# Stick-breaking attention of a head pair: the two heads in step on the two halves of TensorE's rows, float32 value products into one bank, and another split of the eight PSUM banks

## The chip, the cores and the metric

The kernel runs on one core of a Trainium2 chip. The metric is device time in microseconds (us) of one execution; the median of three runs stands for a kernel.

## What is computed

A model of two layers over 528 positions (16 meta tokens and 512 inputs), width 1024. In each layer an input projection feeds three mixers side by side: stick-breaking attention (6 heads of 64), retention (6 heads of 64) and an S5 state-space mixer (256 channels). Their outputs go through one output projection, and a gated feed-forward block of width 2816 follows. The change is about the attention, of which this is the core (per block of 128 queries):

```python
z = jnp.einsum('bhqd,bhkd->bhqk', qb, kb).astype(jnp.float32) * scale
mask = (s_idx[None, :] < t_idx[:, None]) & (s_idx[None, :] >= PAD_FRONT)
log1m = jnp.where(mask, jax.nn.log_sigmoid(-z), 0.0)
between = lax.cumsum(log1m, axis=3, reverse=True) - log1m
w = jnp.where(mask, jnp.exp(jax.nn.log_sigmoid(z) + between), 0.0)
outs.append(jnp.einsum('bhqk,bhkd->bhqd', w.astype(vb.dtype), vb))
```

Everything is float32.

## The kernel before, in words

All activations lie with channels on the 128 partitions and the 528 positions in the free dimension. The large products (input, output and feed-forward projections, tiles `pj`) are made of three matmuls in the reduced type float32r each: both operands are split into a high and a low part (`xh`, `xl`, `wh`, `wl`), and high by high, low by high and high by low are added up in PSUM (`mm3`). With 264 columns each half of the positions has its own bank, so a projection block holds two banks.

The mixers are written as Python generators (`tasks`). After each three matmuls of a projection, `tick` lets up to six tasks take one step, so that mixer work is emitted between projection matmuls; at last Tile's scheduler sets the order on each engine, which is then fixed, and each engine runs its own list in order. Banks are counted by hand: `free` holds a count of banks (`BANKS`, line 32: 5 of the 8) that all mixers share through `banks(n)` and `freed(n)`, and one of attention groups in flight (`GROUPS`, 7). The other three banks are left to the projections. Before the output projection reads a mixer's result, `drain` (line 202) empties the tasks that are still needed; `OUT_PARTS` (line 41) sets which results each third of the output projection reads, and retention is last in both layers.

Attention (`sb_group`, line 816, and `sb_head`, line 857): three pairs of heads per layer; the pair's queries `sq` and keys `sk` are one tile each, head 0 on partitions 0 to 63 and head 1 on 64 to 127. Each head is a lane of its own (`sb_lane(0)`, `sb_lane(1)`, line 1092), and the two lanes run independently of each other. A head's keys and queries fall into three groups: A (272 + 144 + 16 columns), B2 (256 + 144 + 16) and B1 (256 + 256). For a group:

- a bf16 mask product starts the bank `z` (A and B2 only; `identb` is its weight), and float32 matmuls of 64 rows (one head's half of `sk` and `sq`) add the scores;
- ScalarE and VectorE make the softplus `sp`, which is split into `hi` and `lo`; products with `tri` and `ones` (float32r) add the sums over later keys into the same bank;
- ScalarE takes the exponential `e` and frees the bank; `e` is split into `hi` (ScalarE) and `lo` (POOL) by `slow_split`.

The value product `av` of a head takes `hi` and `lo` as two float32r matmuls against a 128-column weight: the 64 columns of the value's high part and the 64 of its low part side by side (`vparts`, line 895, makes them from the transposed values). ScalarE then copies partitions 64 to 127 of the bank (`avl`), VectorE adds them to partitions 0 to 63 into the head's half of `sbo`, and `sbo` is split once more for the output projection.

Retention (`ret_pair`, line 932) also works on a pair: its scores `sc` are float32 matmuls of 64 rows, issued head 0, head 1, head 0, ..., each head in its own bank, and its inner products `ro` are float32 matmuls with 64-column weights, both heads into one bank, also by turns. It takes three banks at once for `sc`, two for `ro`. A head norm (`headnorm`, line 424) takes two banks.

Of the kernel before, what the change touches and what calls it, by code (L numbers as in the profile page):

```python
# [24 lines left out]
NT_SLOTS = 60  # L25
# [6 lines left out]
BANKS = 5  # L32
GROUPS = 7
# [55 lines left out]
def hybrid_kernel(ctx, tc, A, out, dbg=None):  # L89
# [81 lines left out]
    free = {"bank": BANKS, "group": GROUPS}  # L171
# [644 lines left out]
    def sb_group(q, k, r, g, gi, place, hl, ws):  # L816
# [37 lines left out]
        freed(1)  # L854
        ws[gi] = yield from slow_split(e, n, G)

    def sb_head(q, k, v, hh, o):

        r = slice(64 * hh, 64 * hh + 64)
        def weights(groups):  # L860
            hl, ws = {}, {}
            place = {j: (gi, o0, q0) for gi, g in enumerate(groups) for j, q0, q1, o0 in g}
            for gi, g in enumerate(groups):
                spawn(sb_group(q, k, r, g, gi, place, hl, ws), now[0][1])
            return ws

        started = []
        sets = ((G_A,), (G_B2, G_B1))
        yield from take("group", len(sets[0]))
        started.append(weights(sets[0]))  # L870
        for groups in sets:
            ws = started[-1]
            if groups is sets[0]:
                yield from take("group", len(sets[1]))
                started.append(weights(sets[1]))
            yield lambda: len(ws) == len(groups)
# [8 lines left out]
            ws.clear()  # L885
            yield
            freed(len(groups), "group")
            lo = tt("avl")
            SC.copy(out=lo[0:64, :qb - qa], in_=av[64:128, :qb - qa])
            yield  # L890
            V.tensor_tensor(out=o[r, qa:qb], in0=lo[0:64, :qb - qa], in1=av[0:64, :qb - qa], op=ALU.add)
            yield
            freed(1)

    def vparts(vt):

        v = vp.tile([P, 1280], F32R, tag="v", name=nm("v"))
        v4 = v.rearrange("p (j h c) -> p j h c", h=2, c=P)
        for j0, nj in ((0, 4), (4, 1)):
# [5 lines left out]
            pv = ps[:, :P * nj].rearrange("p (j h d) -> p j h d", h=2, d=64)  # L905
            for hh in range(2):
                SC.copy(out=v4[:, j0:j0 + nj, hh, 0:64], in_=pv[:, :, hh, :])
            yield
            for hh in range(2):
                V.tensor_tensor(out=v4[:, j0:j0 + nj, hh, 64:128], in0=pv[:, :, hh, :],  # L910
                                in1=v4[:, j0:j0 + nj, hh, 0:64].bitcast(F32), op=ALU.subtract)
            yield
            freed(1)
        return v4
# [17 lines left out]
    def ret_pair(l, p, q, k, vt, gate, res):  # L932
# [38 lines left out]
        yield from banks(3)  # L971
        pss, ps2 = [bank("sc"), bank("sc")], bank("sc")

        def score(hh, j):
            r, n = slice(64 * hh, 64 * hh + 64), P if j < 4 else NM
            c = slice(P * j, P * j + n)
            mm(pss[hh][:, c] if j < 4 else ps2[:n, :n], lhsT=k[r, c], rhs=q[r, c], start=True, stop=True)

        def kept_last(sc):
            V.tensor_tensor(out=sc[:NM, 512:528], in0=ps2[:NM, :NM], in1=keep[:NM, :NM], op=ALU.mult)  # L980
        score(0, 4)
# [4 lines left out]
        kept_last(scs[0])  # L986
# [3 lines left out]
        score(1, 4)  # L990
        yield
        kept_last(scs[1])
        yield
        freed(3)
# [68 lines left out]
    for l in range(LAYERS):  # L1063
# [15 lines left out]
        def after(n, p, t, l=l, got=got):  # L1079
# [7 lines left out]
            elif n == "sv":  # L1087
                yield lambda: p < 2 or (("done", p - 2, 0) in got and ("done", p - 2, 1) in got)
                t = yield from vparts(t)
            got[n, p] = t  # L1090

        def sb_lane(hh, l=l, got=got, mix=mix):
            for p in range(3):
                yield lambda: all((n, p) in got for n in ("sq", "sk", "sv"))
                if ("sbo", p) not in got:
                    got["sbo", p] = tt("sbo")
                yield from sb_head(got["sq", p], got["sk", p], got["sv", p], hh, got["sbo", p])
                got["done", p, hh] = True
                if ("done", p, 1 - hh) in got:
                    dump(f"sb{l}{p}", got["sbo", p])  # L1100
                    mix[p] = yield from slow_split(got["sbo", p])
# [18 lines left out]
        spawn(sb_lane(0))  # L1120
        spawn(sb_lane(1))
# [160 lines left out]
```

## Time and profile before

| | |
|---|---|
| median of three runs | 1380.3 us (1379.69 to 1380.94) |
| the profiled execution's own time | 1384.1 us |
| its span, first to last instruction | 1382.4 us |
| mean granted TensorE clock | 0.995 |
| busy: PE (matmul) / DVE / ACT / POOL | 1352.0 / 806.3 / 618.1 / 514.6 us |

PE is TensorE's matmuls, PEld its weight loads, DVE VectorE, ACT ScalarE, POOL GpSimd. Matmuls are pipelined: the duration of one reaches into the next ones, so what a matmul costs is read from its start to the next one's start. A float32 matmul shows as two records, a float32r one as one. The rows of the timeline merge equal neighbours: start, time from the first start to the last end, engine, line, operation, output<-inputs, tile shape, count of records.

### The profile page before, as it was taken

The page shows a single profiled execution, that of the slowest core. Times are in us where ns is not written, and L with a number is a line of the kernel's source. Part 1 is how long each engine was busy: PE and PEld are TensorE (multiplying, and loading weights), DVE is VectorE, ACT ScalarE, POOL GpSimd, SP SyncE. Part 2 cuts the span into 40 slices and gives each one's busy share as a digit, 9 for nine tenths or more (in the row PEclk, how much of TensorE's full clock was granted, in tenths as well). Part 3 has the DMA queues.
Part 4 walks back from the last instruction along what each step waited for, and adds up shares of the span by engine and source line. Part 5 has one row for each costly group of instructions (what it writes and reads, how often), then busy time and mean ns, then how long its engine had stood idle before and what let it go on. Part 6 is the DMA issues. An engine that isn't in the chain of part 4 may idle for free.

```text
span 1382.4 us, 22757 instructions
## 1 busy us (share of the span) xinstructions
PE 1352.0 (98%) x9188; PEld 1241.3 (90%) x9188; DVE 806.3 (58%) x1312; ACT 618.1 (45%) x1002; POOL 514.6 (37%) x624
## 2 busy tenths in 40 slices
PE   6999999999899999999999999999999999999998
PEld 6989999999899999999999998998788888888886
DVE  8874858767456445534567386555585543554453
ACT  5456676555252233312354664874354422332231
POOL 5685648322899112201234534562232210220120
PEclk9999999999999999999999999999999999999999
DMA  4221212323221322322232220123232332233223
GB/s 156 70 74 50 78 46 71 94 77 108 84 78 59 109 92 92 92 92 88 78 110 70 71 93 32 70 59 90 86 105 95 102 93 92 92 96 103 92 79 104
DMA packets 38985, 118.27 MB, mean 86 GB/s; under 512 B 4960, under 2 KB 5472, under 8 KB 38880
## 3 DMA queue, kind: packets, MB, share of 16 engines
q1 hardware_dynamic: 38880, 116.82, 25.9%
q8 instruction: 72, 1.18, 0.3%
q14 instruction: 33, 0.27, 0.1%
HBM read 111.46 MB, written 2.10 MB: 82 GB/s over the span
## 4 chain that ended last, share of the span: by engine, by line
PE 75%; DVE 4%; POOL 3%; issue 1%; ACT 1%; SPq 0%; DMA 0%; DVEq 0%; ACTq 0%
PE pj L133 67%; PE z L133 4%; PE ro L133 1%; PE hps L133 1%; PE av L133 1%; PE yps L133 1%; DVE wl L121 1%; DVE y L121 0%; DVE fr L121 0%; POOL st L121 0%; POOL py L121 0%; PE sc L133 0%; POOL gx L121 0%; POOL bb L121 0%; PE rtp L139 0%
## 5 line engine op out<-in xcount | busy, mean ns | idle before, releaser
L133 PE MATMUL pj<-xh,wh 128*128 128x264 f32 (+1 forms) x1792 | 447.8, 310 | 14.6 <-ACT wh L121 5.3
L133 PE MATMUL pj<-xl,wh 128*128 128x264 f32 (+1 forms) x1792 | 450.5, 311 | 1.6 <-DVE xl L121 1.6
L133 PE MATMUL pj<-xh,wl 128*128 128x264 f32 (+1 forms) x1792 | 447.5, 310 | 1.6 <-DVE wl L121 1.6
L121 ACT CAST wh<-wr 128x1024 fp32r<-128x1024 f32 (+3 forms) x209 | 205.9, 987 | 412.7 <-PE pj L133 378.6
L133 PEld LDWEIGHTS pj<-xh,wh 128*128 128x128 f32 x1792 | 296.8, 190 | 33.1 <-issue 7.4
L133 PEld LDWEIGHTS pj<-xl,wh 128*128 128x128 f32 x1792 | 297.2, 190 | 20.2 <-DVE xl L121 2.4
L133 PEld LDWEIGHTS pj<-xh,wl 128*128 128x128 f32 x1792 | 297.0, 191 | 18.7 <-DVE wl L121 1.8
L121 DVE TENSOR_TENSOR wl<-wr,wh 128x1024 fp32r<-128x1024 f32 (+3 forms) x166 | 249.6, 1505 | 72.4 <-ACT wh L121 72.1
L133 PE MATMUL pj<-hi,wh 128*128 128x264 f32 (+1 forms) x720 | 192.5, 322 | 0.0
L133 PE MATMUL pj<-lo,wh 128*128 128x264 f32 (+1 forms) x720 | 192.4, 321 | 0.0
L133 PE MATMUL pj<-hi,wl 128*128 128x264 f32 (+1 forms) x720 | 191.8, 321 | 0.1
L121 POOL TENSOR_TENSOR up<-ga,up 128x528 f32<-128x528 f32 (+1 forms) x44 | 62.0, 1409 | 344.8 <-DVE up L121 344.7
L121 POOL TENSOR_TENSOR wl<-wr,wh 128x1024 fp32r<-128x1024 f32 (+2 forms) x43 | 96.8, 2252 | 137.3 <-ACT wh L121 117.8
L121 DVE TENSOR_TENSOR h<-h,pj 128x264 f32<-128x264 f32 (+1 forms) x144 | 69.4, 510 | 134.7 <-PE pj L133 134.5
L133 PEld LDWEIGHTS pj<-hi,wl 128*128 128x128 f32 x720 | 119.5, 188 | 11.0 <-DVE wl L121 0.5
L133 PEld LDWEIGHTS pj<-hi,wh 128*128 128x128 f32 x720 | 119.4, 188 | 10.9 <-ACT wh L121 0.6
L133 PEld LDWEIGHTS pj<-lo,wh 128*128 128x128 f32 x720 | 119.4, 188 | 10.5
L121 POOL TENSOR_TENSOR lo<-ga,hi 128x528 fp32r<-128x528 f32 (+1 forms) x44 | 59.0, 1340 | 158.3 <-ACT hi L121 158.2
L121 DVE TENSOR_TENSOR up<-pj,R 128x264 f32<-128x264 f32 (+1 forms) x66 | 32.1, 514 | 95.2 <-PE pj L133 95.2
L121 ACT ACTIVATE si<-si,bias 128x528 f32<-128x528 f32 (+1 forms) x44 | 32.1, 730 | 95.3 <-DVE si L121 95.3
L121 DVE TENSOR_TENSOR ga<-si,up 128x528 f32<-128x528 f32 (+1 forms) x44 | 31.7, 719 | 73.8 <-ACT si L121 58.7
L121 POOL TENSOR_TENSOR lo<-sp,hi 128x432 fp32r<-128x432 f32 (+2 forms) x36 | 46.4, 1301 | 34.4 <-ACT hi L121 34.3
(228 smaller groups left out, 1710.9 us busy)
## 6 DMA issues: line engine op xcount, KB each, us to landing
wr<-in_w_in_dram SPq DMA_DIRECT2D x45, 512.0 KB, 3.4
wr<-in_w_gate_dram SPq DMA_DIRECT2D x44, 512.0 KB, 3.4
wr<-in_w_up_dram SPq DMA_DIRECT2D x44, 512.0 KB, 3.4
wr<-in_w_down_dram SPq DMA_DIRECT2D x32, 512.0 KB, 3.5
wr<-in_w_out_dram SPq DMA_DIRECT2D x16, 384.0 KB, 3.2
wr<-in_w_down_dram SPq DMA_DIRECT2D x16, 384.0 KB, 3.1
rc<-in_rope_dram SPq DMA_DIRECT2D x12, 264.0 KB, 3.7
rs<-in_rope_dram SPq DMA_DIRECT2D x12, 264.0 KB, 3.8
```

The lines of the kernel that those rows point to most:

```text
L121: return f(*a, **k)
L133: nc.tensor.matmul(out, lhsT=lhsT, rhs=rhs, start=start, stop=stop, skip_group_check=more)
```

## The change

- **Scores.** `sb_scores` issues both heads' score matmuls by turns, head 0 (rows 0 to 63) into one bank, head 1 (rows 64 to 127) into another. One task per group and pair takes two banks for it, from a count of their own (`ZBANKS` = 4).
- **Value product.** `e` isn't split any more. `av` takes `e` and the values in float32: head 0 with the 64 weight columns that write partitions 0 to 63, head 1 with those that write 64 to 127, by turns, into one bank. The values are copied once as float32 (`by_keys` in place of `vparts`).
- **After it.** The bank holds both heads' rows already; ScalarE copies it as `hi`, VectorE subtracts to `lo`: the split for the output projection comes straight from PSUM, without `avl`, `sbo` and their split.
- **Banks.** `BANKS` 5 to 2 for everything but scores, `ZBANKS` 4, `GROUPS` 7 to 8 (counted per head). Retention's scores take two banks: the last 16 columns of both heads come first, in the same banks, and are read before the others are written.
- **Lanes.** One lane per pair; the next pair may start its groups when the value products of the last one's second set are reached.

```diff
-BANKS = 5
-GROUPS = 7
+BANKS = 2
+ZBANKS = 4
+GROUPS = 8
...
-    def sb_group(q, k, r, g, gi, place, hl, ws):
-
+    def sb_scores(q, k, g):
 
         n = width(g)
-        yield from banks(1)
-        zp = bank("z")
         m = masks.get(n)
+        zs = [bank("z"), bank("z")]
         if m is not None:
-            mm(zp[:, :n], lhsT=identb, rhs=m, start=True, stop=False)
+            for z in zs:
+                mm(z[:, :n], lhsT=identb, rhs=m, start=True, stop=False)
         for j, q0, q1, o0 in g:
-            mm(zp[:, o0:o0 + q1 - q0], lhsT=k[r, KT0[j]:KT0[j] + P], rhs=q[r, q0:q1],
-               start=m is None and j == g[0][0], stop=j == g[-1][0], more=m is None)
+            for hh, z in enumerate(zs):
+                r = slice(64 * hh, 64 * hh + 64)
+                mm(z[:, o0:o0 + q1 - q0], lhsT=k[r, KT0[j]:KT0[j] + P], rhs=q[r, q0:q1],
+                   start=m is None and j == g[0][0], stop=j == g[-1][0], more=m is None)
+        return zs
...
         SC.activation(e[:, :n], z, AF.Exp)
         yield
-        freed(1)
-        ws[gi] = yield from slow_split(e, n, G)
+        freed(1, "scores")
+        ws[gi] = e
...
+            def one(gi, g):
+                yield from take("scores", 2)
+                zs = sb_scores(q, k, g)
+                for hh in range(2):
+                    spawn(sb_group(zs[hh], g, gi, place, hl[hh], ws[hh]), now[0][1])
...
             for n, (gi, (j, q0, q1, o0)) in enumerate(todo):
-                for part in range(2):
-                    mm(av[:, q0 - qa:q1 - qa], lhsT=v[:, j, hh, :], rhs=ws[gi][part][:, o0:o0 + q1 - q0],
-                       start=n == 0 and part == 0, stop=n == len(todo) - 1 and part == 1)
...
+                for hh in range(2):
+                    mm(av[64 * hh:64 * hh + 64, q0 - qa:q1 - qa], lhsT=v[:, P * j + 64 * hh:P * j + 64 * hh + 64],
+                       rhs=ws[hh][gi][:, o0:o0 + q1 - q0], start=n == 0, stop=n == len(todo) - 1)
...
-            lo = tt("avl")
-            SC.copy(out=lo[0:64, :qb - qa], in_=av[64:128, :qb - qa])
-            yield
-            V.tensor_tensor(out=o[r, qa:qb], in0=lo[0:64, :qb - qa], in1=av[0:64, :qb - qa], op=ALU.add)
...
+            SC.copy(out=R_(hi[:, qa:qb]), in_=av[:, :qb - qa])
+            yield
+            V.tensor_tensor(out=R_(lo[:, qa:qb]), in0=av[:, :qb - qa], in1=hi[:, qa:qb], op=ALU.subtract)
...
-    def vparts(vt):
+    def by_keys(vt):
...
+            SC.copy(out=v[:, P * j0:P * (j0 + nj)], in_=ps[:, :P * nj])
...
-        yield from banks(3)
-        pss, ps2 = [bank("sc"), bank("sc")], bank("sc")
+        yield from banks(2)
+        pss = [bank("sc"), bank("sc")]
...
-        spawn(sb_lane(0))
-        spawn(sb_lane(1))
+        for p in range(3):
+            spawn(sb_lane(p))
```

How the order on PE changes, at three places. First, the scores of layer 0's first pair. Before (`z_1055` is one head's group B2, `z_1062` the other's, `z_1067` a group B1):

```order
L133 LDWEIGHTS identb
L133 MATMUL z_1055<-maskB_99,identb 128x416
L133 MATMUL z_1055<-sq_491,sk_494 128x256
L133 MATMUL z_1055<-sq_491,sk_494 128x144
L133 MATMUL z_1055<-sq_491,sk_494 128x16
L133 MATMUL pj_969<-xh_189,wh_796 128x264
L133 MATMUL pj_970<-xh_189,wh_796 128x264
```

Now (`z_913` and `z_914` are the two heads' banks):

```order
L134 LDWEIGHTS identb
L134 MATMUL z_913<-maskB_99,identb 128x416
L134 LDWEIGHTS identb
L134 MATMUL z_914<-maskB_99,identb 128x416
L134 MATMUL z_913<-sq_491,sk_494 128x256
L134 MATMUL z_914<-sq_491,sk_494 128x256
L134 MATMUL z_913<-sq_491,sk_494 128x144
L134 MATMUL z_914<-sq_491,sk_494 128x144
L134 MATMUL z_913<-sq_491,sk_494 128x16
L134 MATMUL z_914<-sq_491,sk_494 128x16
```

The two heads' score matmuls, which stood apart, now alternate. Score matmuls stand in 28 runs before (a run ends where another kind of matmul follows) and in 20 now. Second, a value product of set B. Before, one head:

```order
L133 MATMUL av_1873<-hi_1518,v_598 128x256
L133 MATMUL av_1873<-lo_1519,v_598 128x256
L133 MATMUL av_1873<-hi_1518,v_598 128x256
L133 MATMUL av_1873<-lo_1519,v_598 128x256
L133 MATMUL av_1873<-hi_1454,v_598 128x256
L133 MATMUL av_1873<-lo_1455,v_598 128x256
L133 MATMUL av_1873<-hi_1454,v_598 128x144
L133 MATMUL av_1873<-lo_1455,v_598 128x144
L133 MATMUL av_1873<-hi_1454,v_598 128x16
L133 MATMUL av_1873<-lo_1455,v_598 128x16
```

Now, both heads (`e_1379` and `e_964` are head 0's, `e_1383` and `e_968` head 1's):

```order
L134 MATMUL av_1639<-e_1379,v_594 64x256
L134 MATMUL av_1639<-e_1383,v_594 64x256
L134 MATMUL av_1639<-e_1379,v_594 64x256
L134 MATMUL av_1639<-e_1383,v_594 64x256
L134 MATMUL av_1639<-e_964,v_594 64x256
L134 MATMUL av_1639<-e_968,v_594 64x256
L134 MATMUL av_1639<-e_964,v_594 64x144
L134 MATMUL av_1639<-e_968,v_594 64x144
L134 MATMUL av_1639<-e_964,v_594 64x16
L134 MATMUL av_1639<-e_968,v_594 64x16
```

Ten matmuls for two heads stand in place of ten for one. They stand in 16 runs: in 4 of the 12 sets other work lies between the first matmul of head 0 and the rest. Third, group B1 of layer 0's second pair, now, with projection matmuls around it (`x2`: two equal rows):

```order
L134 MATMUL pj_1746<-xh_194,wh_1474 128x264
L134 MATMUL z_1821<-sq_560,sk_702 128x256 x2
L134 MATMUL pj_1747<-xh_194,wh_1474 128x264
L134 MATMUL pj_1746<-xl_195,wh_1474 128x264
L134 MATMUL pj_1747<-xl_195,wh_1474 128x264
```

Here one head's two matmuls stand alone; the other head's (`z_1822`) follow 22 rows later. Of the 18 groups this is the only one that is wholly apart; in two more B1 groups two of the four matmuls have no partner beside them.

## Rows read from the trace of the kernel before

**Rows 1.** The page: span, busy time per engine, PE and clock in 40 slices.

```profile
span 1382.4 us, 22757 instructions
PE 1352.0 (98%) x9188; PEld 1241.3 (90%) x9188; DVE 806.3 (58%) x1312; ACT 618.1 (45%) x1002; POOL 514.6 (37%) x624
PE   6999999999899999999999999999999999999998
PEclk9999999999999999999999999999999999999999
```

**Rows 2.** Waits of PE: who waited for whom, us in total, times, longest.

```profile
PE pj L133 <- DVE py L121: 2.0, 1, 2.0
PE ro L133 <- DVE sc L121: 1.6, 1, 1.6
PE av L133 <- POOL lo L121: 1.3, 1, 1.3
PE z L133 <- DVE u L121: 0.8, 1, 0.8
```

**Rows 3.** Timeline of PE, groups B2 and B1 of one head.

```profile
190.57 0.49 PE L133 MATMUL pj<-xl,wh 128*128 128x264 f32 x2
190.90 0.35 PE L133 MATMUL z<-maskB,identb 128*128 128x416 bf16 x1
191.18 2.03 PE L133 MATMUL z<-sq,sk 64*128 64x256 f32 x10
193.14 0.51 PE L133 MATMUL pj<-xh,wl 128*128 128x264 f32 x2
193.49 0.41 PE L133 MATMUL pj<-xh,wh 128*128 128x264 f32 x2
193.74 0.28 PE L133 MATMUL pj<-xl,wh 128*128 128x264 f32 x1
```

**Rows 4.** Timeline of PE, group A of one head.

```profile
903.75 1.09 PE L133 MATMUL z<-sq,sk 64*128 64x272 f32 x6
904.77 0.50 PE L133 MATMUL z<-hi,tri 128*128 128x512 f32 x1
```

**Rows 5.** Timeline of PE, retention's scores of both heads by turns.

```profile
254.52 0.41 PE L133 MATMUL pj<-xl,wh 128*128 128x264 f32 x2
254.86 1.30 PE L133 MATMUL sc<-rm,rm 64*16 64x16 f32 x18
256.09 0.51 PE L133 MATMUL pj<-xh,wl 128*128 128x264 f32 x2
```

**Rows 6.** Timeline of PE, seven of retention's inner products by turns.

```profile
260.33 1.09 PE L133 MATMUL ro<-sc,rv 128*64 128x128 f32 x14
261.35 0.71 PE L133 MATMUL ro<-rm,st 128*128 128x128 f32 x4
```

**Rows 7.** Timeline of PE, value products of one head: set A, set B.

```profile
121.72 0.28 PE L133 MATMUL av<-hi,v 128*128 128x272 f32 x1
...
122.33 0.49 PE L133 MATMUL pj<-xl,wh 128*128 128x264 f32 x2
...
131.88 0.28 PE L133 MATMUL av<-hi,v 128*128 128x256 f32 x1
...
132.95 0.49 PE L133 MATMUL pj<-xh,wh 128*128 128x264 f32 x2
```

**Rows 8.** Groups by line: work on e, of ACT and POOL.

```profile
L121 ACT ACTIVATE e<-z 128x512 f32<-128x512 f32 (+2 forms) x72 | 39.2, 546 | 37.3 <-PE z L133 35.7 <-POOL lo L121 0.9
L121 ACT CAST hi<-e 128x432 fp32r<-128x432 f32 (+2 forms) x36 | 20.0, 569 | 0.8
L121 POOL TENSOR_TENSOR lo<-e,hi 128x432 fp32r<-128x432 f32 (+2 forms) x36 | 44.5, 1247 | 31.9 <-ACT hi L121 31.9
```

**Rows 9.** Windows: PE busy, clock, DMA, around the first score products.

```profile
84.20:90.70 6.50, 6.50 (x26) 0.50 0.00 0
```

**Rows 10.** Timeline: layer 0's last head norm, then its result's two parts.

```profile
294.72 1.05 PE L133 MATMUL hps<-hsq,blk 128*128 128x264 f32 x4
300.58 0.64 ACT L121 CAST hi<-o 128x528 fp32r<-128x528 f32 x1 [1.21 <-DVE o L121]
302.02 0.69 DVE L121 TENSOR_TENSOR lo<-o,hi 128x528 fp32r<-128x528 f32 x1
```

More of the change, by code (lines that the diff above doesn't have):

```diff
@@ L24 @@
 HALF = T // 2
-NT_SLOTS = 60
+NT_SLOTS = 62
 AHEAD = 4
@@ L169, in spawn @@
         tasks.append([gen, at, None, None, 0.0])
-    free = {"bank": BANKS, "group": GROUPS}
+    free = {"bank": BANKS, "scores": ZBANKS, "group": GROUPS}
     def take(what, n):
@@ L853, in sb_group, with sb_pair @@
         yield
-        freed(1)
-        ws[gi] = yield from slow_split(e, n, G)
-    def sb_head(q, k, v, hh, o):
-        r = slice(64 * hh, 64 * hh + 64)
+        freed(1, "scores")
+        ws[gi] = e
+    def sb_pair(q, k, v, go, res):
         def weights(groups):
-            hl, ws = {}, {}
+            hl, ws = ({}, {}), ({}, {})
             place = {j: (gi, o0, q0) for gi, g in enumerate(groups) for j, q0, q1, o0 in g}
+            def one(gi, g):
[3 more added lines that the diff above has]
+                    spawn(sb_group(zs[hh], g, gi, place, hl[hh], ws[hh]), now[0][1])
             for gi, g in enumerate(groups):
-                spawn(sb_group(q, k, r, g, gi, place, hl, ws), now[0][1])
+                spawn(one(gi, g), now[0][1])
             return ws
@@ L868, in sb_head @@
         sets = ((G_A,), (G_B2, G_B1))
-        yield from take("group", len(sets[0]))
+        yield from take("group", 2)
         started.append(weights(sets[0]))
+        hi = lo = None
         for groups in sets:
@@ L873, in sb_head @@
             if groups is sets[0]:
-                yield from take("group", len(sets[1]))
+                yield from take("group", 4)
                 started.append(weights(sets[1]))
-            yield lambda: len(ws) == len(groups)
+            yield lambda: all(len(w) == len(groups) for w in ws)
+            if groups is sets[1]:
+                go()
             yield from banks(1)
@@ L904, in vparts @@
             yield
-            pv = ps[:, :P * nj].rearrange("p (j h d) -> p j h d", h=2, d=64)
-            for hh in range(2):
-                SC.copy(out=v4[:, j0:j0 + nj, hh, 0:64], in_=pv[:, :, hh, :])
-            yield
-            for hh in range(2):
-                V.tensor_tensor(out=v4[:, j0:j0 + nj, hh, 64:128], in0=pv[:, :, hh, :],
-                                in1=v4[:, j0:j0 + nj, hh, 0:64].bitcast(F32), op=ALU.subtract)
+            SC.copy(out=v[:, P * j0:P * (j0 + nj)], in_=ps[:, :P * nj])
             yield
             freed(1)
-        return v4
+        return v
     def rotate(t, p, which):
@@ L976, in score @@
             c = slice(P * j, P * j + n)
[L977 to L981, printed above, removed]
+            mm(pss[hh][:n, c if j < 4 else slice(0, n)], lhsT=k[r, c], rhs=q[r, c], start=True, stop=True)
+        for hh in range(2):
+            score(hh, 4)
+        yield
+        for sc, ps in zip(scs, pss):
+            V.tensor_tensor(out=sc[:NM, 512:528], in0=ps[:NM, :NM], in1=keep[:NM, :NM], op=ALU.mult)
+        yield
         for j in range(4):
@@ L1077, in scaled, with after @@
             return t
-        def after(n, p, t, l=l, got=got):
+        def after(n, p, t, l=l, got=got, mix=mix):
             yield
@@ L1087, in after, with sb_lane @@
             elif n == "sv":
-                yield lambda: p < 2 or (("done", p - 2, 0) in got and ("done", p - 2, 1) in got)
-                t = yield from vparts(t)
+                yield lambda: p < 2 or mix[p - 2] is not None
+                t = yield from by_keys(t)
             got[n, p] = t
[L1092 to L1101, printed above, removed]
+        def sb_lane(p, l=l, got=got, mix=mix):
+            yield lambda: all((n, p) in got for n in ("sq", "sk", "sv")) and (p == 0 or ("sb", p - 1) in got)
+            res = []
+            yield from sb_pair(got["sq", p], got["sk", p], got["sv", p], lambda: got.update({("sb", p): True}), res)
+            mix[p] = res[0]
         def ret_lane(l=l, got=got, mix=mix):
```

19 lines of the change are left out of this document (10 added, 9 removed).

## The prediction

> **What bounds the kernel now.** I read the page first: PE is busy for 98% of the span, in every slice after the first few, at full clock nearly throughout [rows 1]. The other engines are at 58% or less, so their work counts only where PE waits for it, and in the stretches with mixers PE waits little: the largest waits there are 2.0, 1.6, 1.3 and 0.8 us [rows 2]. So a change is worth what it takes off the list of PE's matmuls, plus or minus what PE waits. Next I priced matmuls from start to start in the timeline, since their own durations overlap.
>
> Scores of one head: groups B2 and B1 together take 193.14 - 191.18 = 1.96 us, and group A 904.77 - 903.75 = 1.02 us [rows 3, 4], in all 2.98 us for five 256-column matmuls or near it and the small ones. Twelve heads (three pairs, two layers) make 35.8 us. Value products of one head: set A 122.33 - 121.72 = 0.61 us, set B 132.95 - 131.88 = 1.07 us [rows 7], in all 1.68 us, times twelve 20.2 us. These 56 us are what the change rewrites.
>
> **What two halves cost in step.** The kernel has the pattern already, in retention. Sixteen records of 128-column scores, eight matmuls of the two heads by turns, lie in 256.09 - 254.86 = 1.23 us less some 0.14 us for the two 16-column records ahead of them: 1.09 us, 0.14 us for a matmul [rows 5]. The attention's scores, one head alone, cost 1.96 us for 256 + 144 + 16 + 256 + 256 = 928 columns, 2.1 ns a column, 0.27 us for 128 columns [rows 3]. So matmuls on the two row halves, standing beside each other, run at the same time: two for the price of one. For column halves the same: seven inner products of 128 columns take 261.35 - 260.33 = 1.02 us, 0.15 us each [rows 6]. I take it that 256 columns behave as 128 do; no row shows that length in step, and the bounds are no overlap (rival 1) and full overlap.
>
> **The change part by part.**
>
> *Scores.* With full overlap a pair costs what one head did: 6 x 2.98 = 17.9 us. The new order keeps partners apart in one B1 group (two extra matmuls) and half of two more (one extra each): four times 256 columns at 2.1 ns, 2.2 us. So 35.8 becomes 20.1 us: **-15.7 us**. The mask products stay as many as they were.
>
> *Value product.* One float32 matmul with 64 weight columns costs what a score matmul of the same width costs: two records, and rows 6 show 64 columns as quick as rows 5 show 64 rows. The widths are those of the scores, group for group (272 + 144 + 16 and 928 columns). So a pair costs 2.98 us in step, six pairs 17.9 us; four of the twelve sets have their first matmul apart, at 0.54 us each 2.2 us more. That is 20.1 us against 20.2 us: **0**. The float32 matmul takes twice what the two float32r ones took, and the overlap gives it back.
>
> *Entering and leaving a part of the array.* Two projection matmuls that take 0.25 us take 0.34 us just ahead of a run of half-array work (254.86 - 254.52) and 0.35 us just behind one (193.49 - 193.14) [rows 3, 5]: 0.2 us a run beyond the prices above. Score runs go from 28 to 20, value products, which used the full array, now make 16 runs: 8 more runs, **+1.6 us**.
>
> *Work off the other engines.* Gone are the 36 casts of e on ACT (20.0 us) and the 36 subtractions on POOL (44.5 us) [rows 8], the copies and sums of avl and sbo, and sbo's split; new are twelve copies and twelve subtractions out of PSUM and two copies of the values per pair. All of it lies beside PE's projections, so I count it at nothing but for one wait: PE waited 1.3 us for POOL's low part of e ahead of a value product [rows 2], and that part doesn't exist any more: **-1.3 us**. If the cover went, the chain from the exponential to the value product would show; it becomes shorter by 0.57 + 1.25 us per group [rows 8].
>
> *Banks.* 2 + 4 for the mixers leaves two for the projections in place of three, and every mixer but the scores now queues for two banks. In the new order no projection starts on a bank whose reader is close behind: at least 20 matmuls lie between. At the end of layer 0 the last head norm has 73 rows of PE's list ahead of the first matmul that reads its result, before it was 85; at 0.122 us a row that is 8.9 us, and the result's high part was there 301.22 - 294.72 = 6.5 us after the norm [rows 10]. In layer 1 there are 43 rows of 512 columns, longer still. So I count the banks at 0, with waits like those of rows 2 on one side (+8 us, if all four came again and more) and none at all on the other.
>
> *Moved.* The issue order of DMAs on SP's queue moves with the weights alone; nothing of the weights' order changes. Retention's last columns come first now and are one more step before its scores, with the same count of matmuls.
>
> Sum: -15.7 + 0 + 1.6 - 1.3 = -15.4 us. The profiled execution took 1384.1 us and would take 1368.7; the median of the runs is 3.8 us lower, 1380.3 us, which gives **1365 us**.
>
> **Rivals.**
>
> 1. *The halves don't run in step at 256 columns.* Then the scores gain nothing, and the value product costs 12 x 2.98 = 35.8 in place of 20.2 us: +15.6 + 1.6 - 1.3, so **1396 us**. Rows 5 and 6 speak against it; for it, that no row has such a length, and that the operands are twice as long. The Trainium skill (FP8 and Floating Point Precision, TensorE Precision Notes) says that true float32 takes four passes through the array. By that alone, without overlap, this change would lose on the value product.
>
> 2. *The other mixers starve on two banks, and PE waits.* The place: head norms and S5 and retention products of either layer, each of which takes two banks at once and so waits for the one before to be read by ACT or DVE. PE runs its list in order, so one late mixer matmul stops all projection matmuls behind it. The price of one such wait is 0.8 to 2.0 us [rows 2]; the gain is eaten at 15.4 us, some twelve such waits, and beyond that the kernel is slower. At 16 waits of 1.3 us, 20.8 us, **1386 us**. For it speaks that waits of PE for DVE are there already with five banks. Against it, that the order was made with the new counts, and mixer matmuls are spread among the projections as before. The Trainium skill (TensorEngine Tiling (Array Packing), Performance Considerations and Restrictions and Gotchas) warns of both: row tiling raises the pressure on PSUM, since different row tiles need different banks, and tiling speeds up TensorE but not the reading of PSUM. No row here shows a bank shortage so far.
>
> 3. *Half of it comes back as waits.* Both heads' scores are ready at once now, and ACT, which reads each bank twice at 0.55 us and works on e between [rows 8], serves them one after the other; each pair then shows a wait of a us or two. At 6 to 8 us in all, **1372 us**.
>
> 4. *The early stall goes too.* PE waited 2.0 and 0.8 us before the first scores [rows 2], and a stretch of 6.5 us behind that ran at half the clock, 1.2 in place of 2.4 GHz [rows 9], which is worth 3.2 us. If the new order, which brings these scores earlier, avoids both: 6 us more, **1359 us**.
>
> **How the numbers follow.** A measurement of this kernel can tell about 0.2%, 2.8 us, from no change. Forecast (1361 to 1369) 0.60; rival 3 (to 1377) 0.14; rival 4 (from 1355) 0.12; the gain eaten just about, within 2.8 us, 0.04; rival 2 beyond that 0.05; rival 1 0.05. Faster: 0.60 + 0.14 + 0.12 = 0.86; same 0.04; slower 0.10. The range from 1355 to 1377 us takes in the first three and leaves out 0.14.
>
> **What would show it.** In the profile after, PE's score matmuls of a pair should take about 2 us for B2 and B1 of both heads, with records a few ns apart in twos; sets of value products 2.0 and 1.0 us for both heads. PE's busy time should fall by some 15 us with its idle time unchanged. I'm wrong in the main point if records of the two heads follow each other at 0.2 us; wrong on the banks if PE's waits in the stretches with mixers go well over 10 us.

## The result and the profile after

| | before | after |
|---|---|---|
| median of the runs of one chip | 1380.6 us (4 runs) | 1372.2 us (4 runs, 1371.4 to 1373.5) |
| ratio | | 0.9937, 95% interval 0.9923 to 0.9952 |
| the profiled execution's own time | 1384.1 us | 1372.1 us |
| its span | 1382.4 us | 1370.1 us |

The change gains 8.4 us, 0.6%. That is faster, inside the range, and a little over half of the 15.4 us that were forecast. The time is the one that rival 3 gave.

The page of the kernel after (against [rows 1]):

```profile
span 1370.1 us, 22529 instructions
PE 1335.6 (97%) x9188; PEld 1220.8 (89%) x9188; DVE 791.4 (58%) x1270; ACT 589.5 (43%) x936; POOL 464.9 (34%) x588
```

PE is busy for 16.4 us less, and idle for 1370.1 - 1335.6 = 34.5 us where it was 30.4. So the matmuls went as forecast, or better, and part of it came back as waits and, as the table below shows, as half clock. The timeline of PE shows the new price of the scores, at the first pair's groups A and B2, both heads, where rows 3 and 4 have one head:

```profile
67.96 1.10 PE L134 MATMUL z<-sq,sk 64*128 64x272 f32 x12
69.00 0.53 PE L134 MATMUL z<-maskB,identb 128*128 128x416 bf16 x2
69.45 1.07 PE L134 MATMUL z<-sq,sk 64*128 64x256 f32 x12
70.46 0.51 PE L134 MATMUL pj<-xh,wl 128*128 128x264 f32 x2
...
890.68 1.00 PE L134 MATMUL av<-e,v 128*64 128x272 f32 x12
891.61 0.51 PE L134 MATMUL pj<-xh,wh 128*128 128x264 f32 x2
...
894.74 1.83 PE L134 MATMUL av<-e,v 128*64 128x256 f32 x20
896.51 0.51 PE L134 MATMUL pj<-xh,wh 128*128 128x264 f32 x2
```

Group A takes 69.00 - 67.96 = 1.04 us for two heads [rows 4: 1.02 for one], B2 1.01 us. Sets A and B of the value products take 891.61 - 890.68 = 0.93 and 896.51 - 894.74 = 1.77 us for two heads.

For the sums I take a second profile of the kernel before (experiment 1), 1378.9 us and so nearer to its median. Every record of PE is charged from its start to the next one's, less idle time, and less half of what lies in stretches at half clock; those two get rows of their own. "Layer 0" ends where its feed-forward block starts.

| us | before, layer 0 | after, layer 0 | before, rest | after, rest | change |
|---|---|---|---|---|---|
| attention's scores | 18.1 | 11.0 | 18.0 | 9.3 | -15.8 |
| value products | 10.6 | 8.7 | 10.7 | 9.8 | -2.8 |
| retention's scores | 4.1 | 6.2 | 4.2 | 3.8 | +1.7 |
| projections and feed-forward | 243.6 | 246.0 | 897.0 | 896.9 | +2.3 |
| all other matmuls | 69.4 | 67.8 | 67.9 | 67.2 | -2.3 |
| PE idle behind its first matmul | 15.5 | 20.0 | 3.9 | 5.8 | +6.3 |
| lost to half clock | 3.2 | 6.8 | 1.7 | 1.6 | +3.6 |
| sum | 364.6 | 366.6 | 1003.4 | 994.4 | -7.0 |

The matmuls cost 16.9 us less and 9.9 us came back. And by these two profiles it came back in one place: **layer 0 is no faster at all**, the rest gains 9.0 us. The timelines say the same in one row each. The first feed-forward matmul of layer 0, before (second profile):

```profile
369.71 0.36 PE L133 MATMUL pj<-xh,wh 128*128 128x264 f32 x1 [3.75 <-DVE ga L121]
```

and after:

```profile
371.61 0.56 PE L134 MATMUL pj<-xh,wh 128*128 128x264 f32 x1 [3.78 <-DVE ga L122]
```

These are single profiles, and they scatter. In the first profile of before the same matmul starts at 372.98 us: by that one layer 0 gains 1.4 us and the rest 10.9 us. So that most of the gain lies behind layer 0 holds by either, and that layer 0 gains nothing only by one. Half clock scatters most: the first profile of before lost 6.8 us to it, the second 4.9 us. By the granted clocks of all runs on record, an average of 6.9 us went to it before (73 runs) and 8.9 us after (4 runs), so of the 3.6 us in the table about 2 us are the change's.

Here are PE's waits, from the timelines (in brackets the idle time ahead and what ended it). After:

```profile
28.95 0.52 PE L134 MATMUL pj<-xh,wl 128*128 128x264 f32 x2 [3.19 <-DVE wl L122]
...
77.44 0.39 PE L134 MATMUL pj<-xh,wh 128*128 128x264 f32 x1 [2.52 <-ACT we L122]
...
85.64 0.66 PE L140 MATMUL vps<-ident,sv 128*128 128x128 f32 x4 [0.83 <-DVE u L122]
...
87.83 0.39 PE L134 MATMUL pj<-xh,wh 128*128 128x264 f32 x1 [1.16 <-DVE sq L122]
...
187.49 0.36 PE L134 MATMUL pj<-xh,wh 128*128 128x264 f32 x1 [0.69 <-DVE ysm L122]
...
280.19 0.51 PE L134 MATMUL pj<-hi,wh 128*128 128x264 f32 x2 [0.44 <-ACT hi L122]
281.96 0.51 PE L134 MATMUL pj<-lo,wh 128*128 128x264 f32 x2 [1.26 <-DVE lo L122]
...
773.55 0.69 PE L134 MATMUL hps<-hsq,blk 128*128 128x264 f32 x2 [0.97 <-DVE ysm L122]
...
970.25 0.62 PE L134 MATMUL ro<-sc,rv 128*64 128x128 f32 x6 [0.87 <-DVE sc L122]
```

Before, second profile:

```profile
28.91 0.51 PE L133 MATMUL pj<-xh,wl 128*128 128x264 f32 x2 [1.62 <-DVE wl L121]
...
70.54 0.63 PE L139 MATMUL wps<-ident,ws 128*128 128x128 f32 x4 [0.51 <-DVE py L121]
74.02 0.56 PE L133 MATMUL pj<-xh,wh 128*128 128x264 f32 x1 [2.00 <-DVE py L121]
...
218.26 0.38 PE L133 MATMUL av<-lo,v 128*128 128x256 f32 x1 [1.30 <-POOL lo L121]
```

The first row of each shows a wait that costs nothing: PE goes on at 28.9 us in both, when VectorE has the weight, however early PE got there. Its growth, 1.6 us, stands in the 6.3 us of the table all the same. The stall of the first scores is no new one either: PE waited 0.5 + 2.0 us for VectorE at 70 to 74 us before, and waits 2.5 us for ScalarE at 77 us now. The wait for POOL's `lo` is gone, as forecast. New are the two for VectorE's `u` and `sq`, S5's result (`hi`, `lo` at 280 to 282 us), and smaller ones. Behind three of them the clock was at half, 1.2 in place of 2.4 GHz (windows of the kernel after: stretch, length, busy time of PE, PEld, VectorE, ScalarE and POOL, granted clock, DMA share, GB/s):

```profile
77.90:81.30 3.40, 3.40 (x18) 3.40 (x17) 3.40 (x9) 2.13 (x5) 3.40 (x6) 0.50 0.02 5
88.10:91.50 3.40, 3.40 (x17) 3.40 (x17) 3.31 (x4) 1.98 (x3) 3.40 (x5) 0.50 0.00 0
282.70:286.10 3.40, 3.40 (x18) 3.40 (x17) 0.64 (x3) 0.41 (x2) 0.00 (x0) 0.50 0.26 90
```

PE is busy for all of each, so each costs half its length, 1.7 us. The second profile of before has one between 29 and 370 us, behind its wait at 74 us; in the first one that stretch is twice as long [rows 9].

### The profile page after: what moved, and what is told of

It reads as the page before. It is cut to its first block, busy times and chain, and to the rows that moved or that the text cites. A ratio compares the mean times of both kernels' runs of the same rounds, so it can differ in the third digit from the quotient of the medians.

```text
span 1370.1 us, 22529 instructions
## 1 busy us (share of the span) xinstructions
PE 1335.6 (97%) x9188; PEld 1220.8 (89%) x9188; DVE 791.4 (58%) x1270; ACT 589.5 (43%) x936; POOL 464.9 (34%) x588
## 4 chain that ended last, share of the span: by engine, by line
PE 82%; DVE 10%; POOL 3%; ACT 1%; issue 1%; DMA 1%; SPq 0%; DVEq 0%; ACTq 0%
PE pj L134 71%; PE z L134 5%; DVE ysm L122 2%; PE hps L134 1%; PE av L134 1%; PE ro L134 1%; DVE wl L122 1%; DVE s5w L122 1%; PE kps L134 1%; PE sc L134 1%; DVE gg L122 1%; DVE st L122 0%; DVE py L122 0%; POOL py L122 0%; DVE sp L122 0%
## 5 line engine op out<-in xcount | busy, mean ns | idle before, releaser
L134 PE MATMUL pj<-xh,wh 128*128 128x264 f32 (+1 forms) x1792 | 454.4, 311 | 16.8 <-ACT wh L122 5.1
L134 PE MATMUL pj<-xh,wl 128*128 128x264 f32 (+1 forms) x1792 | 453.3, 310 | 3.2 <-DVE wl L122 3.2
```

The costliest lines, as they stand in the source:

```text
L134: nc.tensor.matmul(out, lhsT=lhsT, rhs=rhs, start=start, stop=stop, skip_group_check=more)
```

## Was the profile of before a typical one?

Experiment 1: the kernel before, unchanged.

> The kernel before, unchanged, profiled once more. The profiled execution of it that the sum was made against took 1384.1 us, 3.8 us over the median of the runs. If those 3.8 us were waits and half-clock time of that one execution (theory), this profile comes out near 1380.5 us, with PE's waits or its half-clock time 3 to 4 us smaller and its matmul work the same within 0.5 us. If the profiler itself costs 3.8 us (rival), it is at 1384 again.

Measured: 1378.9 us, span 1377.2 us, 5.2 us less than the first profile: 1.9 us of idle time, 2.0 us of half clock, 1.1 us of matmul work (0.5 was allowed) and 0.2 us at the start. The rule of the prediction, to sum against the profile and then take off its 3.8 us, was sound. Fifteen runs of it beside these experiments lay between 1377.8 and 1384.6 us.

## Do the halves run in step, and what does the order have to do with it?

Experiment 2, scores head by head:

```diff
-        for j, q0, q1, o0 in g:
-            for hh, z in enumerate(zs):
+        for hh, z in enumerate(zs):
+            for j, q0, q1, o0 in g:
```

> The changed kernel with one edit: all score matmuls of head 0 of a group are issued ahead of those of head 1, instead of by turns. Theory (the two heads run at the same time on the two row halves only when they stand beside each other): the scores go back from 20.3 to some 36 us of PE's list, so 1372 + 15 = 1387 us, slower than the kernel before by 0.5 %. Rival (the gain of the change comes from elsewhere, or the chip overlaps matmuls a few places apart as well): 1372 to 1376 us.

Measured: 1374.9 us, only 2.7 us more. Neither number of the theory held; the time is in the range of its rival, by which matmuls a few places apart overlap as well. The timeline has the first groups A and B2 as

```profile
67.18 1.66 PE L134 MATMUL z<-sq,sk 64*128 64x272 f32 x12
...
69.23 1.61 PE L134 MATMUL z<-sq,sk 64*128 64x256 f32 x12
```

From start to start that is 1.60 and 1.54 us: neither the 1.04 of taking turns nor the 2.04 of two heads one after the other [rows 4, twice]. All scores cost 26.9 us, so of the 15.8 us saved turns make 6.6 us, and standing one behind the other already makes 9.2 us. The single records tell how: head 1's first record (272 columns) starts at 67.752 us, 6 ns behind head 0's first one of 144 columns, though three records of head 0 that stand ahead of it in PE's list start at 67.868, 67.991 and 68.019 us. It passes them, on the other half of the rows. In group B2 three records are passed in the same way, and in a group B1, with only two matmuls a head, that is enough for full overlap:

```profile
877.26 1.14 PE L134 MATMUL z<-sq,sk 64*128 64x256 f32 x8
878.33 0.51 PE L134 MATMUL pj<-xl,wh 128*128 128x264 f32 x2
```

Both heads take 878.33 - 877.26 = 1.07 us, though issued head by head, and 1.06 us by turns. In this run 3.5 us less went to half clock than in the profile after, which is why only 2.7 of the 6.6 us show in the time. The granted clocks of all its runs (0.995 to 0.996, after the change 0.992 to 0.994) say the same; why is open.

Experiment 3, value products head by head:

```diff
-            for n, (gi, (j, q0, q1, o0)) in enumerate(todo):
-                for hh in range(2):
+            for hh in range(2):
+                for n, (gi, (j, q0, q1, o0)) in enumerate(todo):
```

> The changed kernel with one edit: all value products of head 0 of a set are issued ahead of those of head 1. Theory (float32 costs twice as much, and the step of the two column halves gives it back): the value products go from 18.5 to some 34 us, so 1372 + 15 = 1387 us. Rival (float32 with 64 weight columns is no dearer than the two float32r products were, overlap or not): 1372 to 1376 us.

Measured: 1384.2 us, 1.0029 of before (1.0016 to 1.0042). The products cost 28.5 us in place of 18.5, less than the 34 us expected for the same reason as above: in the set A at 165.90 us head 1's first record starts at 166.414 us, 6 ns behind head 0's first one of 144 columns and ahead of three of head 0's (166.530, 166.653 and 166.681 us). The kernel is slower than before. So rival 1 is settled: the halves do run in step at 256 columns, on rows and on columns, and without it the float32 products would lose.

Experiments 4 and 8, the scores part alone, with the value path of before (`e` split, two float32r products for each head, `avl`, `sbo` and its split):

```diff
-        ws[gi] = e
+        ws[gi] = yield from slow_split(e, n, G)
...
-                t = yield from by_keys(t)
+                t = yield from vparts(t)
```

> The changed kernel with the value path of the kernel before: e split into hi and lo, values split, two float32r products with 128 weight columns for each head, avl, sbo and its split; scores in step, banks, lanes as in the change. The prediction had the float32 value product at 0, so by it this kernel is at 1372 to 1374 us (PE might wait 1.3 us for a low part of e). If the value product's part of the change saved 2.8 us of PE's list, as the profiles of before and after have it, and its shorter chain saved waits as well: 1375 to 1380 us. If the copies and subtractions that the float32 path puts on VectorE and ScalarE are what makes PE wait more after the change (rival): below 1372 us.

> The scores part of the change alone, once more (value path of the kernel before), now with three banks for the mixers and two for the scores. With two and four it took 1419 us, with 53 us of waits where the full change has 26. If the longer value path is too much for two banks (it holds a bank for each head, and ScalarE and VectorE have to empty them): with three banks the waits fall to 20 to 30 us, 1375 to 1390 us. If the waits come from the longer chain behind the exponential itself, casts and subtractions on ScalarE and POOL with both heads at once: 1410 us or more again.

Measured: 1419.1 us with two and four banks, far above every range expected, and 1391.9 us with three and two, just above the lower range; both slower than before. PE's idle time was 53.2 and 36.2 us, and 23.5 and 20.2 us went to half clock. Two waits of the first, in its timeline:

```profile
291.87 3.10 PE L134 MATMUL sc<-rm,rm 64*128 64x128 f32 x16 [6.81 <-DVE sc L122]
...
314.27 0.81 PE L134 MATMUL pj<-hi,wh 128*128 128x264 f32 x2 [7.08 <-ACT hi L122]
```

The first is an effect of the change's edit to retention: its scores now wait until VectorE has read the 16 columns out of the same bank, and VectorE had 14 `ysm` instructions ahead of that (6.41 us). The matmul work was 1331 and 1325 us (1327 after the change, 1344 before). So in these two splits of the banks the value product part, which I had put at 0 on PE, is what lets the scores part pay: without it the saved matmul time and more comes back. With three and two banks the whole change takes 12.4 us less (experiment 7). Both kernels have the change's lanes and its retention as well; the scores with the old value path and retention on three banks were not tried.

## Is it the banks?

Experiment 7, three banks for the mixers and two for the scores:

```diff
-BANKS = 2
-ZBANKS = 4
+BANKS = 3
+ZBANKS = 2
```

> The changed kernel with three banks for the mixers and two for the scores (five in all, as before the change), in place of two and four. Theory B (the mixers starve on two banks): PE's waits fall from 25.5 us towards the 20 us of the kernel before, 1364 to 1368 us. Theory A: the waits that the trace names are for ScalarE's and VectorE's queues, not for a bank, so the banks change them little: 1370 to 1376 us; with two score banks the second group of a pair waits for the first one's exponential, which would lengthen attention's chain and could add waits.

Measured: 1379.5 us, 0.9994 of before (0.9979 to 1.0008). That is above both ranges expected. With five banks in all, the projections have three again, as before the change. Yet the waits rose to 31.3 us, and the first pair's place got no better (one wait of 4.6 us, where the change has 2.5, 0.8 and 1.2 us):

```profile
80.56 1.09 PE L140 MATMUL wps<-ident,ws 128*128 128x128 f32 x4 [4.63 <-DVE u L122]
```

Rival 2 in its plain form falls: a third bank for the mixers, taken from the scores, doesn't shorten the waits, and the split of two and four is worth 7 us. Waits are only a part of that (5.5 us between the profiles): the value products cost 23.2 us in place of 18.5, because in all twelve sets other work stands between the first matmul and the rest.

## The waits of layer 0

Theory A: the waits at 77 to 88 us come from other engines' lists, where attention's first groups meet S5's parameter work, and S5's result is late at 280 us. ScalarE's timeline after the change:

```profile
71.44 1.07 ACT L122 COPY we<-wps 128x512 f32<-128x512 f32 x2 [5.35 <-PE wps L140]
72.40 1.79 ACT L122 ACTIVATE e<-z 128x432 f32<-128x432 f32 x4
74.03 1.06 ACT L122 ACTIVATE e<-e 128x432 f32<-128x432 f32 x2
74.94 1.08 ACT L122 CAST wh<-wr 128x1024 fp32r<-128x1024 f32 x1
75.87 1.04 ACT L122 ACTIVATE e<-e 128x416 f32<-128x416 f32 x2
76.76 0.62 ACT L122 COPY we<-wps 128x512 f32<-128x512 f32 x1
```

PE needs the bank that the last row empties, and its projection starts at 77.44 us. Ahead of it stand the passes over four score groups, two of each head. VectorE's timeline shows the second place:

```profile
79.58 2.34 DVE L122 TENSOR_TENSOR st<-st 128x4 f32<-128x4 f32 x1
...
84.64 0.60 DVE L122 SCALAR_TENSOR_TENSOR sp<-z,e 128x432 f32<-128x432 f32 x1
85.16 0.76 DVE L122 TENSOR_TENSOR u<-pj,R 128x264 f32<-128x264 f32 x2
85.84 1.59 DVE L122 SCALAR_TENSOR_TENSOR sp<-z,e 128x432 f32<-128x432 f32 x3
87.35 0.42 DVE L122 TENSOR_TENSOR sq<-pj,R 128x264 f32<-128x264 f32 x1
```

Until 84.64 us it is at S5's phasors (`py`, `st`, `phr`, `phi`); `u` and `sq`, the copies that free projection banks, come behind them and between the softplus of both heads. Five kernels tested the theory. First, experiments 5 and 6, S5's two input projections earlier in layer 0's list, ahead of all (`"uu000111222333344445555"`) or behind the first pair (`"000uu111222333344445555"`):

```diff
-PROJ = ("000111uu222333344445555", "uu000333311122244445555")
+PROJ = ("uu000111222333344445555", "uu000333311122244445555")
```

> The changed kernel with the two S5 input projections first in layer 0's list, not seventh and eighth. Theory A (the new waits come from the first attention groups meeting the S5 parameter work of VectorE and ScalarE at 70 to 90 us, and from S5's result being late at 280 us): the waits of 2.5, 0.8, 1.2 and 0.4 + 1.3 us go, and two or three of the half-clock stretches behind them, 1.7 us each; 1372 less 6 to 11 is 1361 to 1366 us. Theory B (two banks for all mixers but the scores make PE wait): no less wait in all, 1370 to 1375 us. Against both: S5 now waits for its parameters itself, and if its products stop PE at 60 to 100 us the time goes above 1375.

> The changed kernel with the two S5 input projections behind the first pair of heads (fourth and fifth), not seventh and eighth. Theory A: the wait for S5's result at 280 us goes (1.7 us and a half-clock stretch of 1.7 us), that of the first scores at 77 us stays: 1368 to 1371 us. Theory B: 1370 to 1375 us.

Measured: 1390.8 and 1387.6 us. Both numbers missed. `sv`, whose copies free two more projection banks, now stood in VectorE's list behind phasors (PE waited for it 3.8 us at 77 us and 8.3 us at 83 us). At the layer's end PE waited 3.6 us at 305 us for retention in the one, and 7.1 us at 294 us for S5's result in the other, although its inputs had come earlier. Next, experiment 9, the phasors of layer 0 on POOL, both halves:

```diff
-            eng = engines[hf]
+            eng = G
```

> The changed kernel with both halves of the S5 phasors of layer 0 on POOL, where before the change and after it one half is on VectorE (70.9 to 84.6 us, in VectorE's queue ahead of the copies that empty the projections' banks and of the softplus of the first scores). Theory A (PE's waits of 2.5, 0.8 and 1.2 us at 77 to 88 us come from VectorE's queue being full of that work while the four score banks are held): they go, 4.5 us, and with them one or two half-clock stretches of 1.7 us: 1364 to 1368 us. Rival C (ScalarE's queue, which has both heads' score passes ahead of the copies out of the wps banks, is what holds PE at 77 us): the 2.5 us stay and only the other two go, 1369 to 1372 us. If S5 then gets its phasors too late, the wait for its result at 280 us grows and 1372 to 1380 us comes out.

experiment 10, the first pair's attention held back until the parameters are made:

```diff
-            yield lambda: all((n, p) in got for n in ("sq", "sk", "sv")) and (p == 0 or ("sb", p - 1) in got)
+            yield lambda: all((n, p) in got for n in ("sq", "sk", "sv")) and (p == 0 or ("sb", p - 1) in got) and bool(par)
```

> The changed kernel, with the first pair's attention in layer 0 held back until the S5 parameters are made (some 20 us later). Theory A: no wait at 77 to 88 us, 4.5 us and up to 3.4 us of half clock less; attention's results come later, and if the output projection of layer 0 has to wait for the third pair the time is above 1372 us by that wait. Without it 1365 to 1368 us; with it up to 1385 us. Rival B (two banks for the other mixers) expects no fall: 1372 us or more.

and experiment 11, ScalarE's passes over the first pair's scores 4 us later:

```diff
+        late = 4000 if l == 0 and p == 0 else 0
...
-                    spawn(sb_group(zs[hh], g, gi, place, hl[hh], ws[hh]), now[0][1])
+                    spawn(sb_group(zs[hh], g, gi, place, hl[hh], ws[hh]), now[0][1] + late)
```

> The changed kernel with the first pair's score passes of ScalarE in layer 0 emitted 4 us later in the program's own model of time, nothing else: ScalarE's list then has the two copies out of the wps banks ahead of the four score passes, where the change has them behind eight instructions of attention and one cast (72.4 to 76.8 us). VectorE's softplus of these groups stands behind the phasors until 84.6 us in any case. If rival 3 of the prediction is the cause at this place (ScalarE serves both heads' scores, and the copies that free PE's banks come after), PE's wait of 2.5 us at 77 us falls below 1 us, and the 0.8 and 1.2 us at 85 and 88 us, which hang on VectorE, stay: 1368 to 1371 us where the half-clock stretch goes as well. If the wait is one of banks (two for the mixers but the scores) or of VectorE, it stays at 2.5 us and the time at 1372 us. If the list further down is put in another order by it, and retention or S5 come late at 250 to 310 us: 1375 to 1385 us, with the wait at 77 us gone nevertheless.

Measured: 1382.9, 1385.7 and 1382.6 us (1.0024, 1.0043 and 1.0022 of before), all slower than before; the first two lie above every range expected, the third in its last one. Two of them did at their place what the theory says. With the phasors on POOL the two waits for VectorE are gone, and this one stays:

```profile
77.69 0.39 PE L134 MATMUL pj<-xh,wh 128*128 128x264 f32 x1 [2.27 <-ACT we L122]
```

With ScalarE's passes later that one falls to 0.55 us, and VectorE's takes over:

```profile
76.42 0.39 PE L134 MATMUL pj<-xh,wh 128*128 128x264 f32 x1 [0.55 <-ACT we L122]
...
84.14 0.59 PE L134 MATMUL pj<-xh,wh 128*128 128x264 f32 x1 [5.03 <-DVE u L122]
```

So the 2.5 us belong to ScalarE's list (rival 3 of the prediction, rival C here) and the 0.8 and 1.2 us to VectorE's phasors. But no time came of it: between 250 and 300 us PE then waited for retention and S5, 8.4 us in six waits with the phasors on POOL, and 5.2 us at 291 us for S5's result with the later passes. With attention held back, the place itself didn't clear: PE waited 2.2 us for VectorE's `u` at 78 us, and 3.5 us at 174 us and 3.7 us at 255 us besides. Against the profile after, the three kernels have 7.5, 8.0 and 9.2 us more idle time of PE and 4.9, 7.1 and 5.3 us more of half clock, nearly all in layer 0. In these three lists what was put off early came back later in the layer, with half clock on top.

Last, the end itself, experiment 12: the second half of S5's gate product ahead of the first one's sigmoid.

```diff
+            gs.append(g)
             yield
             freed(2)
-            sigmoid(g, g, 1.0)
+        for m, g in enumerate(gs):
+            sigmoid(g, g, 1.0)
```

> The changed kernel with one more change, late in each layer's mixers: the second half of S5's gate product is made before the sigmoid of the first half, not after it, so that the chain glu, sigmoid, product, hi, lo of the second half (275.8 to 282.5 us in the profile after the change) starts some 4 us earlier. Theory A for this place (S5's result is late, 0.4 + 1.3 us at 280 to 282 us, and the half-clock stretch behind it costs 1.7 us): both waits go and the stretch with them, layer 0's feed-forward block starts up to 3.4 us earlier than 371.6 us, and the time is 1368.5 to 1371 us. If the lost time of layer 0 sits in the retention chain behind it, which ends last in any case, the wait moves to the last third of the output projection and the time stays at 1371 to 1374 us. Nothing ahead of 265 us should differ.

Measured: 1372.4 us (six runs, 1369.7 to 1376.6), 0.995 of before (0.9936 to 0.9965). Its profiled execution took 1369.7 us:

```profile
279.31 1.16 PE L134 MATMUL kv<-rv,kt 128*128 128x128 f32 x8 [0.62 <-ACT kt L122]
...
366.71 0.36 PE L134 MATMUL pj<-xh,wh 128*128 128x264 f32 x1 [3.77 <-DVE ga L122]
```

The waits for `hi` and `lo` are gone, the half-clock stretch behind them too, and the layer ends 371.6 - 366.7 = 4.9 us earlier. Two stretches of half clock fewer in layer 0 make some 3.4 us of that, and one of the two, at 88 us in the profile after, is not the edit's doing: PE's list is the same in both up to 270 us. This execution was also the fastest of the six. The rest of the program took 1368.0 - 366.7 = 1001.3 us, after the change 1370.1 - 371.6 = 998.5: the edit moved layer 1's list as well, where two groups' scores lost their partners (10.6 us of scores in place of 9.3). The two waits went as the theory for this place says; by its time the version can't be told from the change, and its median lies in the range of the other reading (1371 to 1374 us). None of the twelve kernels beats the change by more than the runs' spread.

## Why the prediction was right and wrong

- **Scores, -15.7 us: right** (-15.8). The reason, too, with one correction: the halves run at the same time when both have work waiting close by (three records apart in experiments 2 and 3), not only when they take turns.
- **Value product, 0: too small a gain.** It saved 2.8 us. Sets A and B take 0.93 and 1.77 us for two heads where 1.0 and 2.0 were reckoned, and what was priced at 20.2 us before costs 21.3 when counted from start to start. The larger miss is in what it does for the other engines: experiments 4 and 8 show that without it, in their bank splits, the scores part is lost.
- **Entering and leaving part-array runs, +1.6 us: right in size.** Projection matmuls directly ahead of and behind part-array work cost 5.5 us more than the same number of them among themselves before (second profile) and 7.4 us more after: 1.9 us. A part of it is retention's, whose scores stand in 16 runs where they stood in 12; the sum didn't have that. The rest of the 2.3 us in the table is within what the profiles of before differ by (1.0 us).
- **"The same count of matmuls" in retention: wrong.** The scores kept their count and lost their partners. They now wait for VectorE to read the 16 columns out of the same bank, and in two of layer 0's three pairs the scheduler put the heads apart. The timeline of PE after the change, against [rows 5]:

```profile
199.95 1.16 PE L134 MATMUL sc<-rm,rm 64*128 64x128 f32 x8
201.03 0.39 PE L134 MATMUL pj<-xh,wh 128*128 128x264 f32 x1
201.35 1.16 PE L134 MATMUL sc<-rm,rm 64*128 64x128 f32 x8
```

  One head's eight records cost 201.03 - 199.95 = 1.08 us, as much as both heads' sixteen did [rows 5: 1.09]. Twice that is the 2.1 us of layer 0 in the table. The order of the changed kernel's matmuls has it, and the prediction didn't use it.
- **"So I count the banks at 0", waits -1.3 us: this step failed.** The wait for POOL went, and 7.6 us others came, 6.3 us net, of which 1.6 us at 28.9 us cost nothing; half clock adds 3.6 us by these profiles and some 2 us by all runs. Rival 3 had the mechanism at its largest place: ScalarE's passes over both heads' scores stand ahead of the copies that free PE's banks. The Trainium skill (TensorEngine Tiling (Array Packing), Performance Considerations) says that tiling speeds up TensorE and not the emptying of PSUM; at this place the trace agrees. That the time is the one rival 3 gave is luck in good part. It expected such a wait for each of the six pairs; only layer 0's first pair has one, and PE waited as long there before, for VectorE. The waits that are new come from elsewhere: VectorE's phasors hold the next banks (0.8 and 1.2 us), S5's result is late (1.7 us), and 0.7 to 1.0 us each at 187, 774 and 970 us. A third bank for the mixers didn't shorten them.
- **Rival 4, the early stall goes: the other way.** The stall stayed, at 2.5 us, and two more waits stand behind it.
- By layers the forecast of 15.4 us, some 7.7 us a layer, was beaten in the rest of the program (9.0 us, or 10.9 against the first profile of before) and failed in layer 0 (2.0 us slower, or 1.4 us faster). The attention runs there beside S5's parameter work, which layer 1 has behind it already. That this is the cause is argued and not shown: the kernels that moved the two apart gained nothing.

Left open: VectorE's phasors are held up by POOL's part of a weight at the same place (last section), and a kernel that moves that part elsewhere was not tried. Retention's scores on three banks again, beside the rest of the change, was not tried, nor were the edits of experiments 9, 11 and 12 together. Nor is it shown why the same wait (1.26 us for S5's `lo`) has a half-clock stretch behind it in the profile after and none in experiment 2.

## What to carry to other kernels

Reckon a saving on the bounding engine stage by stage: here the time saved came through whole where the other engines' lists were short, and much of it came back as waits and half clock where they were long. Before costing a shared bank at nothing, read in each reader's list what stands ahead of the instruction that empties it. And look up in the changed order whether matmuls that should run side by side still stand side by side, or near enough. Before a difference of a few us between two profiles is explained, see how much two profiles of one kernel differ.

## What the runs showed of the hardware

- A matmul on one half of the rows can start ahead of three records of the other half that stand before it in PE's list (67.752 against 67.868, 67.991 and 68.019 us, experiment 2). So can one on a half of the columns (166.414 against 166.530, 166.653 and 166.681 us, experiment 3), and in all the groups looked at, A, B2 and B1 of the scores and sets A and B of the values, it is three. That PE runs its list in order, as the description of the kernel and the prediction have it, holds here except for those three records. The Trainium skill (TensorE: Matmul & The Clock Gate, The mechanism) says that matmuls start strictly in the program's order; these traces show otherwise for two row halves and two column halves, and the measurement decides.
- One VectorE subtraction of four columns, 0.15 us elsewhere, took 2.34 us at 79.58 us (above), while POOL was at this one:

```profile
79.26 2.63 POOL L122 TENSOR_TENSOR wl<-wr,wh 128x1024 fp32r<-128x1024 f32 x1
```

  That puts 2.2 us on VectorE's list just where PE waits for its end. Both profiles of the kernel before have it too (2.34 us at 75.56 and at 74.84 us), so the change didn't bring it. In experiments 10 and 11 other small products of the phasors take 2.37 us at 74.77 us and 2.50 us at 78.29 us beside such a subtraction, ahead of PE's waits for `u`. In the whole profile after, 83 VectorE instructions take over 0.6 us more than the median of their kind, 97 us in all, and 81 of them start beside a POOL instruction and last at least to its end. The Trainium skill (SBUF — State Buffer, SBUF: two separate sides) has VectorE and GpSimd exclude each other from a shared pair of ports for a whole instruction when VectorE's has two SBUF inputs; the trace agrees. With the phasors on POOL (experiment 9) VectorE's softplus, with one input from PSUM, ran beside such a subtraction of 2.39 us undelayed, three in 1.59 us.
